# A batched matmul on one core: Tile's schedule against one critical section with waits by hand and a loop on TensorE

## The chip, the core and the metric

The kernel runs on one core of a Trainium2 chip. The metric is the time of one execution on the device in microseconds (us), the median of several runs. The profile is of one such execution; its span goes from the first instruction to the last.

## The reference

```python
batch, m, k, n = 32, 512, 1024, 768      # x: batch x m x k, weight: batch x k x n, float32

def reference(x, weight):
    return np.matmul(x, weight).astype(np.float32)
```

Each of 32 batches has its own x (512 x 1024) and its own weight (1024 x 768). There are 67 MB of x, 101 MB of weight and 50 MB of output in main memory, all in fp32.

## The kernel before

**The data.** A weight is cast to bf16 on its way in and lands as `w_sb` (128 partitions, 8 rows of 768 each; `load_w`, line 70). x lands in bf16 as well, two batches in one transfer (`load_pair`, line 60), so that 64 partitions hold one batch and 64 the other. Batch 0 and batch 31 are alone. Batch 0's x stays in fp32: three of its four row blocks come in one transfer of 1.5 MB on SP's queue (line 169, `x_first`). The fourth (`x_fourth`, 0.5 MB) comes in 18 transfers, four of 16 rows, two of 2 rows and twelve of 5 rows (line 172); the DMA completion semaphores make SP wait between them, so that they are issued from 1.2 to 29.3 us. There are four weight buffers, three x buffers (batch 0's `x_first` has one of them) and three output buffers. Batch 31's x is loaded by `load_last` (line 64).

**The work on a batch.** The contraction index must lie on the partitions, so TensorE (PE) first transposes x against an identity matrix, two bf16 values at a time as one fp32 word (`words`, line 78; `transpose_first`, line 113, for batch 0). VectorE (DVE) copies the result from the accumulator memory and sorts it by batch (`transpose_pair`, line 96; lines 93 and 94 for the last pair, 101 for batch 31, 115 for batch 0). A pair of batches has 8 groups of 4 transposes, with two accumulator buffers `pt` between PE and DVE. All 8 groups come ahead of the matmuls of the pair's first batch.

Then come 64 matmuls a batch (`matmuls`, line 132): for each of 4 row blocks, 8 steps of the contraction, each with 512 and 256 output columns. Two row blocks fill three accumulator banks (`pm`); there are two sets of three. When two row blocks are done, `evacuate` (lines 151 to 163) copies the banks to the output buffer: ScalarE (ACT) the first and the third, DVE the second, each in two halves of 64 partitions. A stored pair of batches, 3 MB, is one transfer.

**The one batch in parts.** `CHUNKED` holds batch 28 alone. Its weight comes in two transfers of half the contraction each, and its matmuls go through all four row blocks with the first half before they go through them with the second, in all six banks at once.

**The order.** The schedule is written out by hand (`manual_schedule`): the program order of each engine is that of the code, and the framework places the waits. Pool's queue issues all loads but the first x, and most stores. At batch b it issues, for odd b, the load of the pair that is three batches ahead and the store of an older pair, and for every b the weight of batch b+3, as soon as PE is done with batch b-1. The last stores (pairs 12 to 15) come late: two on Pool at batch 28, the others on SP at the very end, in halves for batches 30 and 31.

## Time and profile before

| | |
|---|---|
| median of 3 runs | 513.84 us (513.78 to 513.95) |
| the profiled execution | 513.74 us |
| its span | 511.9 us |
| PE busy | 425.1 us, 83% of the span |
| DVE, ACT busy | 171.8 and 145.4 us |
| TensorE clock granted, mean | 0.953 |
| HBM read, written | 167.77 and 50.33 MB, 426 GB/s over the span |
| queue of the Pool-issued transfers | 96.4% of 16 engines' span |
| first matmul of batch 0; of its last row block | 15.8 us; 45.9 us |

The slices in the DMA row are fortieths of the span, 12.8 us each, and a digit is the busy share in tenths, 9 for 90% or more. The GB/s row counts the bytes on the side of the core's memory: a load that casts fp32 to bf16 counts half of what is read. The clock row gives what the throttle granted to TensorE. A landing time runs from issue to the completion semaphore. In a timeline, the bracket behind a group is the idle time just ahead of it and what ended it.

### The profile page before, as it was taken

How to read it: one execution, taken by the hardware profiler on the slowest of the kernel's cores; microseconds unless marked ns; L12 is line 12 of the kernel's file. 1: busy time of each engine (PE TensorE's matmuls, PEld its weight loads, DVE VectorE, ACT ScalarE, POOL GpSimd, SP SyncE). 2: the span in 40 equal slices, each digit the busy share in tenths (PEclk: the TensorE clock that was granted, in tenths of full speed). 3: DMA queues.
4: the chain of work that ended last, by engine and by line, in shares of the span. 5: the costliest groups of instructions: out<-in, count | busy, mean ns of one | idle time of the engine just before them, and what ended most of it. 6: DMA issues, size and time to landing. Idle time of an engine off the chain costs nothing.

```text
span 511.9 us, 5954 instructions
## 1 busy us (share of the span) xinstructions
PE 425.1 (83%) x2528; PEld 276.6 (54%) x2576; DVE 171.8 (34%) x272; ACT 145.4 (28%) x249; POOL 34.3 (7%) x69
## 2 busy tenths in 40 slices
PE   1804998989898989997888878887888879898992
PEld 1503666665656665653656446464465645666661
DVE  0302426253525252431525315252152621615230
ACT  1200242414242423332242322323223232232310
POOL 3000010101010101000010000101001000010000
PEclk9956999999999999997999989999799998999997
DMA  8999999999999999999999999999999999999997
GB/s 238 224 222 214 220 217 217 335 221 317 235 223 331 216 327 229 230 325 220 329 224 242 313 223 333 217 253 300 219 338 215 266 289 219 333 219 217 325 428 338
DMA packets 10218, 135.65 MB, mean 265 GB/s; under 512 B 1232, under 2 KB 1232, under 8 KB 2128
## 3 DMA queue, kind: packets, MB, share of 16 engines
q0 software_dynamic: 9072, 126.88, 96.4%
q1 hardware_dynamic: 1120, 8.39, 4.1%
q8 instruction: 20, 0.33, 0.2%
q14 instruction: 6, 0.05, 0.0%
HBM read 167.77 MB, written 50.33 MB: 426 GB/s over the span
## 4 chain that ended last, share of the span: by engine, by line
PE 45%; DMA 37%; issue 9%; DVE 5%; another core or an unknown queue 1%; POOL 0%; SPq 0%; ACT 0%; POOLq 0%
PE pm L132 40%; DMA w_sb<-in_weight_dram 29%; DMA one_sb<-in_x_dram 8%; PE pt L78 5%; DVE xT L96 3%; DVE out_sb L163 1%; PE pt L113 0%; DVE xT L93 0%; POOL out_dram L182 0%; DVE xT L94 0%; DVE one_sb L155 0%; DVE xT L101 0%; ACT out_sb L156 0%; SPq L172 0%
## 5 line engine op out<-in xcount | busy, mean ns | idle before, releaser
L132 PE MATMUL pm<-w_sb,xT 128*128 128x256 bf16 (+1 forms) x2000 | 343.8, 330 | 24.8 <-DMA w_sb<-in_weight_dram 22.3
L132 PEld LDWEIGHTS <-xT 128*128 128x128 bf16 x2048 | 203.3, 99 | 160.6 <-issue 33.0
L163 ACT COPY out_sb<-pm 64x512 f32<-64x512 f32 x240 | 139.5, 581 | 339.4 <-PE pm L132 286.1
L163 DVE COPY out_sb<-pm 64x512 f32<-64x512 f32 x120 | 82.6, 688 | 267.7 <-PE pm L132 185.9
L78 PE MATMUL pt<-ident,x_sb 128*128 128x128 f32 x496 | 79.9, 302 | 21.7 <-DVE xT L96 19.7
L78 PEld LDWEIGHTS pt<-ident,x_sb 128*128 128x128 f32 x496 | 69.3, 209 | 32.9 <-DVE xT L96 27.7
L96 DVE COPY xT<-pt 128x1024 bf16<-128x1024 bf16 x112 | 72.2, 687 | 10.6 <-PE pt L78 10.2
L70 POOL DMA_DIRECT2D w_sb<-in_weight_dram x33 | 17.7, 536 | 403.0 <-PE pm L132 402.2
L113 PE MATMUL pt<-ident,one_sb 128*128 128x128 f32 x8 | 1.9, 422 | 20.5 <-DMA one_sb<-in_x_dram 20.5
L115 DVE CAST xT<-pt 128x256 bf16<-128x256 f32 x16 | 6.0, 441 | 35.3 <-PE pt L113 35.1
L113 PE MATMUL pt<-ident,x_sb 128*128 128x128 f32 x24 | 4.9, 363 | 10.9 <-DMA x_sb<-in_x_dram 10.4
L113 PEld LDWEIGHTS pt<-ident,one_sb 128*128 128x128 f32 x8 | 1.6, 218 | 20.8 <-issue 20.8
L113 PEld LDWEIGHTS pt<-ident,x_sb 128*128 128x128 f32 x24 | 3.9, 206 | 11.7 <-issue 10.4
L60 POOL DMA_DIRECT2D x_sb<-in_x_dram x15 | 8.1, 540 | 11.0 <-PE pt L113 11.0
L182 POOL DMA_DIRECT2D out_dram<-out_sb x14 | 7.5, 538 | 5.7 <-issue 4.8
L155 DVE COPY out_sb<-pm 128x512 f32<-128x512 f32 x2 | 1.4, 692 | 8.8 <-PE pm L132 8.8
L155 DVE COPY one_sb<-pm 128x512 f32<-128x512 f32 x2 | 1.4, 692 | 8.3 <-PE pm L132 8.3
L93 DVE COPY xT<-pt 128x512 bf16<-128x512 bf16 x8 | 3.4, 421 | 0.7 <-PE pt L78 0.7
L94 DVE COPY xT<-pt 128x512 bf16<-128x512 bf16 x8 | 3.3, 415 | 0.0
L154 ACT COPY out_sb<-pm 128x512 f32<-128x512 f32 x2 | 1.2, 587 | 6.5 <-PE pm L132 6.5
L101 DVE COPY xT<-pt 128x1024 bf16<-128x1024 bf16 x4 | 2.6, 685 | 0.2 <-PE pt L78 0.2
L156 ACT COPY one_sb<-pm 128x512 f32<-128x512 f32 x2 | 1.2, 587 | 4.2 <-PE pm L132 4.2
(10 smaller groups left out, 5.1 us busy)
## 6 DMA issues: line engine op xcount, KB each, us to landing
w_sb<-in_weight_dram POOLq DMA_DIRECT2D x31, 1536.0 KB, 40.2
out_dram<-out_sb POOLq DMA_DIRECT2D x14, 3072.0 KB, 51.3
x_sb<-in_x_dram POOLq DMA_DIRECT2D x15, 2048.0 KB, 47.1
out_dram<-out_sb SPq DMA_DIRECT2D x1, 3072.0 KB
x_sb<-in_x_dram SPq DMA_DIRECT2D x1, 1536.0 KB
w_sb<-in_weight_dram POOLq DMA_DIRECT2D x2, 768.0 KB, 50.4
out_dram<-one_sb SPq DMA_DIRECT2D x2, 768.0 KB
out_dram<-out_sb SPq DMA_DIRECT2D x2, 768.0 KB
```

The source lines that it names most:

```text
L60: nc.gpsimd.dma_start(out=xs[b], in_=pair_view[b // 2])
L70: nc.gpsimd.dma_start(out=ws[b][:, at:at + n, :], in_=w_view[b, :, at:at + n, :])
L78: nc.tensor.transpose(pt[:, j, :], pairs[:, mo, j::JT], ident)
L93: nc.vector.tensor_copy(both[:, 0, :, half], pt[:, :, 0])
L94: nc.vector.tensor_copy(in_rows[1][:, :, half::2, :], pt[:, :, 1])
L96: nc.vector.tensor_copy(both[:, :, :, half].rearrange("p b j i r -> p j b i r"), pt)
L113: nc.tensor.transpose(pt[:, i, :], rows[:, JT * h + i::KT], ident)
L115: nc.vector.tensor_copy(xT[:, 2 * h + j].rearrange("p (h i) r -> p r h i", h=2), pt[:, 2 * j:2 * j + 2].rearrange("p r (i h) -> p r h i", ...
L132: nc.tensor.matmul(pm[bank][:, at:at + size], xT[:, ko // 2, :, ko % 2], ws[b][:, ko, off:off + size], start=(ko == 0 and not (together an ...
L155: nc.vector.tensor_copy(o[:, 512:1024], pm[1])
L163: copy(mine[:, at:at + 512], pm[i][H * h:H * (h + 1)])
L182: nc.gpsimd.dma_start(out=two_view[at], in_=twos[at])
```

## The change

The whole program becomes one critical section, in which the framework places no waits; semaphores, buffers and waits are allocated and written by hand. In it:

- PE runs batches 1 to 28 in a loop of seven passes on the engine itself (`pe.Fori`), each over two pairs of batches. Batch 0, the last pair (29 and 30) and batch 31 stand outside. The other engines stay written out. Because a loop needs waits on constants, PE takes its counters down (`then_inc(s, -1)`, and -16 and -8 at the end of a pass), and SP waits for each landing and then raises one counter for weights and one for x (`landed`).
- `x_first` holds all four row blocks and comes in one transfer of 2 MB into the space of the third output buffer.
- `CHUNKED` is gone: weight 28 comes in one transfer and its batch runs like the others.
- There are two x buffers and not three, so the load of pair k waits until PE has transposed pair k-2.
- The third bank's copy is shared: ACT copies its first half, DVE its second (`out_on_dve`, last line).
- bf16 matmuls are given whole, with no separate weight load in the listing.
- The order of loads and stores on Pool and SP is the old one.

```diff
-    CHUNKED = {B - 4: (4, 4)}
+    GROUPS = 2 * MT
+    W_SLOTS, X_SLOTS, OUT_SLOTS = 4, 2, 3
+    LOOPS = (B - 4) // W_SLOTS
+    LOOPED = 2 * LOOPS
...
+    x_first = outs[2][:, :MT * K].rearrange("p (mo k) -> p mo k", mo=MT)
...
+    def load_w(b):
+        if b >= W_SLOTS:
+            pool.wait_ge(s_mm, mm_done(b - W_SLOTS))
+        pool.dma_start(out=ws[b % W_SLOTS], in_=w_view[b]).then_inc(s_w[b % W_SLOTS], 16)
+
+    def load_x(k):
+        if k >= X_SLOTS:
+            pool.wait_ge(s_pt, pt_done(k - X_SLOTS))
...
+    def take(s):
+        pe.wait_ge(s, 1).then_inc(s, -1)
+
+    def pair_on_pe(k, q):
+        b = 2 * k + 1
+        take(s_xr)
+        for g in range(GROUPS):
+            if GROUPS * q + g > 1:
+                pe.wait_ge(s_c, GROUPS * q + g - 1)
+            transpose(b, g)
+        for r in range(2):
+            take(s_wr)
+            for mt in range(MT):
+                at = 4 * q + 2 * r + mt // 2
+                if not r:
+                    pe.wait_ge(s_c, GROUPS * q + 2 * mt + 2)
+                pe.wait_ge(s_a, at + 1 + mt % 2)
...
+                    pe.wait_ge(s_d, at + 1 + mt % 2)
+                multiply(b + r, mt)
...
+        with pe.Fori(0, LOOPS):
+            for q in range(2):
+                pair_on_pe(q, q)
+            pe.wait_ge(s_c, 2 * GROUPS).then_inc(s_c, -2 * GROUPS)
+            pe.wait_ge(s_a, 9).then_inc(s_a, -8)
+            pe.wait_ge(s_d, 9).then_inc(s_d, -8)
+        pair_on_pe(LOOPED, 0)
...
+    def out_on_dve(b, p):
...
+        for piece in pieces(b, p, 1):
+            last = dve.tensor_copy(*piece)
+        last.then_inc(s_d, 1)
+        dve.tensor_copy(*pieces(b, p, 2)[1]).then_inc(s_dp, 1)
...
+    def landed(what, i):
+        slots, ready = what
+        sp.wait_ge(slots[i % len(slots)], 16 * (i // len(slots) + 1))
+        sp.sem_inc(ready, 1)
...
-        x_first = x_pool.tile([P, MT - 1, K], F32, name="x_sb")
-        x_fourth = one_pool.tile([P, 1, K], F32, name="one_sb")
-        nc.sync.dma_start(x_first, x_view[0, :, :MT - 1])
-        few = [slice(at, first + 20, 4) for first in (0, 20, 40) for at in range(first, first + 4)]
-        for rows in (slice(64, 80), slice(80, 96), slice(96, 112), slice(112, P), slice(60, 62), slice(62, 64), *few):
-            nc.sync.dma_start(x_fourth[rows, 0], x_view[0, rows, MT - 1])
...
+    with tc.tile_critical():
+        sp.dma_start(x_first, x_view[0]).then_inc(s_first, 16)
+        on_pool()
+        on_pe()
+        on_dve()
+        on_act()
+        on_sp()
+        clear_on_pool()
```

`clear_on_pool` waits for the stores issued by Pool and for SP to have issued the last one, and then resets the section's semaphores.

## The prediction

> **What bounds the kernel now.** I read the page first (the DMA row, the queues, the groups), then the chain that ended last in order of time, then the timelines of PE and SP around the end, and last the table by windows around PE's long waits.

> The page:

> ```profile
> DMA  8999999999999999999999999999999999999997
> GB/s 238 224 222 214 220 217 217 335 221 317 235 223 331 216 327 229 230 325 220 329 224 242 313 223 333 217 253 300 219 338 215 266 289 219 333 219 217 325 428 338
> q8 instruction: 20, 0.33, 0.2%
> x_sb<-in_x_dram POOLq DMA_DIRECT2D x15, 2048.0 KB, 47.1
> w_sb<-in_weight_dram POOLq DMA_DIRECT2D x2, 768.0 KB, 50.4
> ```

> The transfer engines are full from end to end. Slices of loads alone run at 217 GB/s (counted in the bf16 that lands), so one weight (1.573 MB) takes 7.25 us, one pair of x (2.097 MB) 9.7 us, and a stored pair (3.146 MB at twice the rate) 7.3 us: a pair of batches needs 2 x 7.25 + 9.7 + 7.3 = 31.5 us. x waits 47 us from issue to landing, so some 37 us of other work stand ahead of it in the queue.

> The chain of waits:

> ```profile
> 77.33 0.70 DVE out_sb L163
> 104.53 0.70 DVE out_sb L163
> ...
> 373.37 49.45 DMA w_sb<-in_weight_dram
> 422.81 0.14 issue
> 422.95 8.34 PE pm L132 x40
> ```

> With its data there, PE takes 104.53 - 77.33 = 27.2 us a pair, so it gains 4.3 us a pair on the transfers until it has caught up, near 230 us. From then on it waits for a weight, the last time at 422.95, for batch 26. After that it never waits for a transfer again.

> The timelines, PE and SP:

> ```profile
> 422.95 12.24 PE L132 MATMUL pm<-w_sb,xT 128*128 128x512 bf16 x63 [4.14 <-DMA w_sb<-in_weight_dram]
> 441.43 20.96 PE L132 MATMUL pm<-w_sb,xT 128*128 128x512 bf16 x125
> 462.23 1.12 PE L78 MATMUL pt<-ident,x_sb 128*128 128x128 f32 x8
> 498.46 5.53 SPq L232 DMA_DIRECT2D out_dram<-out_sb  x2
> ```

> Batches 27 and 28 run from 441.43 to 462.39 without a gap, 10.48 us each, so batch 28 starts at 451.9. The last store is issued at 503.66, and the packets of the stores end at 510.6. Alone, it would start 1.0 us after its issue (as the first x does, issued at 0.74, first packet at 1.75) and move 0.786 MB at the 428 GB/s of slice 39 in 1.9 us: done by 506.6. So the end is still the transfers', and PE's tail has **4.0 us of cover**.

> The table by windows, around two waits of PE:

> ```profile
> 326.00:331.00 5.00, 2.58 (x16) 1.58 (x17) 1.15 (x2) 1.15 (x2) 1.60 (x3) 1.00 1.05 221
> 422.00:428.00 6.00, 5.05 (x22) 2.68 (x23) 0.00 (x0) 0.63 (x2) 0.00 (x0) 0.72 1.00 214
> ```

> After a gap of 2.47 us (325.95 to 328.42) the clock stays at 1.00. After each of the four gaps of 3.9 to 4.5 us it falls, and batch 26 takes 12.1 us instead of 10.48: 1.6 us lost. In two of the four the half clock lasted twice as long, so a long gap costs 1.6 to 2.7 us.

> **The change, part by part.** The sum is made against the profiled execution: span 511.9, 513.74 in all, 0.1 below the median of 513.84.

> *First x in one transfer.* The bytes are the same. In the transfer records the twelve 5-row pieces fall on five of the 16 engines (11 or 12 packets of 4 KB there until 100 us, at most two on most of the others), while the first three instruction fetches fall on other engines. So in before each of 11 engines carries 4 rows of x_fourth and about 20/11 fetches of 0.93 us, each of the five some 16 rows. In after every engine carries 8 rows: +4 x 0.16 = 0.6 us on the 11, less on the five. PE can start at about 16 us (first x by 11, weight 0 by 15) instead of 44; that only means that it meets the transfers' pace at batch 4 instead of at 230 us, since weights cannot come sooner.

> *TensorE's loop.* The instruction fetches are 20 packets for 5,100 PE records, one per 256. The loop body has 640 of them and some 50 waits, 2.7 packets. Not shown by any run: whether a pass after the first fetches them again. If not, about 5 packets remain (the text is 1,300 long); if so, 7 x 3 to 7 x 5 plus 4, up to 39. On the 11 engines with 0.6 for x this gives (5 - 20) x 0.93/11 + 0.6 = -0.7 us, -1.0 with the present unevenness gone (the engines end from 507.9 to 510.6), and +1.2 with 27 packets (+2.2 with 39). I take **+1.2**, and keep both ends. The stall of a branch back has no row either. It is covered twice: the waits ahead of the branch are met when DVE has copied a bank 1.4 us into the last 5.2 us of matmuls, so up to 3.8 us of work are queued, and PE idles some 3.4 us a pair. If both covers are too small, PE only comes later to a weight, until 20 us of queued transfers are used up. The last branch back lies before batch 25; the exit falls through.

> [...]

> *Two x buffers.* The load of x for pair k+2 now waits for the transposes of pair k. In before it was issued at 326.77 for the pair transposed from 340 to 345.4, so it moves 19 us later, and on Pool the store and the weight of batch b+3 queue behind it, 6 us later than now (339.28 to about 346). The order in the queue is unchanged, and of the 37 us ahead of x 18 are left. Cost: nothing; once the cover is gone, one us per us, in every pair.

> *DVE takes half of the third bank.* Ahead of a pair's transposes DVE now copies three half banks instead of two: +0.69 us a pair (its L163 mean is 688 ns). Hidden while PE waits for weights (27.2 + 0.7 = 27.9 against 31.5), but on the path once after batch 28: **+0.7**.

> *No weight in parts.* The two halves of weight 28 were issued at 402.30 and 402.83 and landed 50.4 us later in the middle, that is at 453.0; they lie 3.6 us apart, so the second landed at about 454.8 and PE can act on it 0.2 to 0.5 us later. Before, batch 28 began at 451.9 on the first half. Now it waits for the whole: 455.3 - 451.9 = **+3.4**. The stretch before it is DMA paced, 31.5 - 27.9 = 3.6 us of waiting, between the 2.47 that keeps the clock and the 3.88 that loses it. A fallen clock costs **0 or 2.2** (middle of 1.6 and 2.7).

> *Waits by hand.* SP relays each landing to PE: +0.1 (its semaphore records take 17 to 28 ns, two hops). PE's other waits are met a half batch ahead. Entry and exit of the section each add a round of all engines; the round at the end of before takes 0.8 us (511.1 to 511.9), the one at the start under 0.1 beyond its slowest engine: 0 to 1.0, taken as +0.5. Pool's clearing lies beside the last stores.

> **The sum.** The last store is late by 1.2 + 3.4 + 0.7 + 0.1 = 5.4 us; 4.0 are covered; 1.4 remain, and 0.5 for the rounds: 1.9. The transfers' own path gives 1.2 to 1.4 + 0.5, the same. 513.84 + 1.9 = **515.7 us**. The terms' bounds carry this case from 514.7 to 516.9.

> **Rivals.**

> - *The clock falls ahead of batch 28* (fetches repeated): +2.2, 517.9. For it: 3.6 us is nearer to 3.88 than to 2.47. Against: a stall at the branch before batch 25 shortens the wait for 26 and shifts nothing at 28, and if the clock falls at 26 the wait at 28 shrinks to 2.
> - *The loop stays on the engine* (5 fetches, even engines), the case on the other side: the term is -1.0, so the last store is late by 3.2, within the cover. The transfers' own work ends 1.5 to 2.3 us sooner (ends at their mean, 509.2, less 15 x 0.93/16 = 0.9), but the last store ends at 506.6 + 3.2 = 509.8, 0.8 sooner than now, and 0.5 goes to the rounds: 513.84 - 0.3 = 513.5, no change. It decides where fetches stay below 13. With the clock's fall it gives 515.7.
> - *Weight loads no longer run ahead.* The listing of after shows no separate weight load beside a bf16 matmul. If each of a pair's 128 matmuls showed its 99 ns, a pair would cost 27.9 + 12.7 = 40.6 us, 9 over the transfers' pace: some 650 us. Against it: the transposes carry their loads in the same way, 209 ns each, and eight take 1.12 us, 140 ns each, so the load lies under the matmul before it.
> - *The transfer queue runs dry* behind the later x: decides at 18 us of PE delay, which nothing here brings; a gap of 2 us a pair would be 540.

> **How the numbers follow.** Fetches repeated 0.55 (clock kept 0.33, fallen 0.22), loop resident 0.39 (clock kept 0.23, fallen 0.16), the last two together 0.06. A measurement of this kernel can tell 0.2%, 1.03 us, from no change. Faster by more takes a quarter of the resident case with the clock kept, 0.06 (rounds at nothing and weight 28 early); the same takes the rest of it, 0.17, a fifth of the resident case with the clock fallen, 0.03, and a fifth of the forecast, 0.07; slower is left, 0.67. The range leaves out the last two rivals and the outer ends: 513.0 to 518.2.

> **What would show it.** Right: the DMA row full to the end; PE starting near 16 us and idle some 3.5 us at every even batch; a wait of 3 to 4 us for w28 near 452, where before has none; DVE's first spread of a pair 0.7 us later; the last store issued at 508 to 509. The count of instruction packets decides the loop (5, 20 or over 25), the PEclk of the window 450 to 460 the clock. Wrong: a DMA share under 1.0 between 20 and 500 us, a pair's matmuls over 21 us, or a last store before 505.

## The result, and the profile after

The changed kernel takes 514.77 us (median of 20 runs, 513.8 to 516.19), the kernel before 513.87 beside it (20 runs, 513.77 to 514.18). The ratio is 1.0016, 95% interval [1.0009, 1.0022]. So it is slower by 0.9 us, half of the 1.9 forecast, inside the forecast range, and its runs scatter over 2.4 us where those of before scatter over 0.4 (in the three groups of experiments below, before itself scatters over 1.4 to 1.5 us, 513.72 to 515.25). The interval leaves out 1, so the 0.16% is more than noise, but it lies just under the mark of 0.2% that the chances used, and the interval reaches over that mark. By the mark the result counts as the same, to which the forecast gave 0.27; slower had 0.67. The profiled execution took 515.67 us.

The page of the changed kernel: span, granted clock, transfer engines and the queue of instruction fetches.

```profile
span 513.5 us, 6063 instructions
PEclk9999999899998889999889999999899898898999
DMA  8999999999999999999999999999999999999995
q8 instruction: 5, 0.08, 0.1%
```

The transfer engines are as full as before (38 of the 40 digits are a 9 on both pages). Five instruction packets, not 20: they fall at 31, 55, 79, 478 and 495 us, so the first pass of the loop (its transposes begin at 31.1 us, those of the second at 87.2) fetched its body and the six after it fetched nothing.

The waits of PE (total, times, longest):

```profile
PE pt L153 <- DVE xT L233: 30.0, 35, 1.9
PE pm L134 <- PEq L157: 29.9, 13, 3.6
```

The first line holds the gap ahead of each pair's transposes, up to 1.9 us (before 1.0). The second is the wait for a weight at the even batches, from 1.2 to 3.6 us (PEq is PE's sequencer, which waits there for SP's word that the weight has landed).

The timeline of PE at the end (start, length, matmuls; in the bracket the idle time ahead and what ended it; 64 matmuls are a batch):

```profile
443.89 10.35 PE L134 MATMUL pm<-w,xT 128*128 128x256 bf16 x62
455.49 10.56 PE L134 MATMUL pm<-w,xT 128*128 128x512 bf16 x63 [1.25 <-PEq L157]
465.89 1.12 PE L153 MATMUL pt<-ident,x 128*128 128x128 f32 x8
468.93 1.41 PE L153 MATMUL pt<-ident,x 128*128 128x128 f32 x8 [1.92 <-DVE xT L232]
470.53 3.77 PE L153 MATMUL pt<-ident,x 128*128 128x128 f32 x16 [0.18 <-DVE xT L232]
474.44 20.75 PE L134 MATMUL pm<-w,xT 128*128 128x256 bf16 x125
```

Three lines of the same timeline of before, for the gaps ahead of the transposes of pairs 13 and 14 and the start of batch 29:

```profile
437.18 1.35 PE L78 MATMUL pt<-ident,x_sb 128*128 128x128 f32 x8 [1.03 <-DVE xT L96]
464.51 1.38 PE L78 MATMUL pt<-ident,x_sb 128*128 128x128 f32 x8 [1.17 <-DVE xT L94]
469.05 20.96 PE L132 MATMUL pm<-w_sb,xT 128*128 128x512 bf16 x125
```

The timeline of SP's queue at the end of the changed kernel:

```profile
503.99 5.46 SPq L115 DMA_DIRECT2D out_dram<-out  x2
```

Batch 28 starts at 455.49, 3.6 us later than before (451.9). The gap ahead of pair 14's transposes is 1.92 us (before 1.17), and the 16 transposes from 470.53 take 3.77 us because the clock is down (0.50 from 470.95 to 474.36 us in the trace's clock records). Batches 29 and 30 end 5.2 us later than before (474.44 + 20.75 = 495.19 against 469.05 + 20.96 = 490.01; by a missing record the start reads 0.2 too late). SP's last group, which issues the last two stores, ends at 509.45 instead of 503.99: 5.46 us late.

The table by windows (span, PE, weight loads, DVE, ACT, POOL, granted clock, DMA share, GB/s) says where the clock fell:

```profile
450.00:460.00 10.00, 8.70 (x54) 5.11 (x53) 3.06 (x5) 2.90 (x5) 1.60 (x3) 1.00 1.00 212
469.00:475.00 6.00, 5.67 (x28) 4.46 (x30) 4.89 (x14) 0.00 (x0) 0.00 (x0) 0.72 1.04 219
```

At full clock behind the wait for weight 28, where the forecast's rival put a fall; down at the transposes, where nothing was expected.

### The profile page after: what moved, and what is told of

Its sections match the earlier page's. It is cut to its first block, busy times and chain, and to the rows that moved or that the text cites. A ratio compares the mean times of both kernels' runs of the same rounds, so it can differ in the third digit from the quotient of the medians.

```text
span 513.5 us, 6063 instructions
## 1 busy us (share of the span) xinstructions
PE 430.2 (84%) x2528; PEld 280.2 (55%) x2576; DVE 209.6 (41%) x332; ACT 110.2 (21%) x189; POOL 33.7 (7%) x68
## 3 DMA queue, kind: packets, MB, share of 16 engines
q0 software_dynamic: 8928, 126.88, 96.1%
## 5 line engine op out<-in xcount | busy, mean ns | idle before, releaser
L134 PE MATMUL pm<-w,xT 128*128 128x256 bf16 (+1 forms) x2000 | 338.8, 328 | 32.8 <-PEq L157 29.9
L134 PEld LDWEIGHTS pm<-w,xT 128*128 128x128 bf16 x2048 | 202.2, 99 | 168.0 <-issue 40.8
L279 DVE COPY out<-pm 64x512 f32<-64x512 f32 x120 | 82.6, 689 | 252.4 <-PE pm L134 251.5
L265 ACT COPY out<-pm 64x512 f32<-64x512 f32 (+1 forms) x122 | 70.7, 580 | 300.6 <-PE pm L134 299.9
L153 PE MATMUL pt<-ident,x 128*128 128x128 f32 x496 | 87.3, 326 | 32.6 <-DVE xT L233 30.0
L153 PEld LDWEIGHTS pt<-ident,x 128*128 128x128 f32 x496 | 73.7, 210 | 45.6 <-DVE xT L233 39.3
L268 ACT COPY out<-pm 64x512 f32<-64x512 f32 (+1 forms) x62 | 35.8, 578 | 89.2 <-PE pm L134 89.2
L281 DVE COPY out<-pm 64x512 f32<-64x512 f32 x60 | 41.2, 686 | 0.0
L101 POOL DMA_DIRECT2D x<-in_x_dram x15 | 8.0, 532 | 274.0 <-PE pt L153 273.8
L92 POOL DMA_DIRECT2D w<-in_weight_dram x32 | 17.2, 538 | 125.6 <-PE pm L134 124.6
L153 PE MATMUL pt<-ident,out 128*128 128x128 f32 x32 | 6.9, 371 | 12.7 <-DMA out<-in_x_dram 12.5
L109 POOL DMA_DIRECT2D out_dram<-out x14 | 7.5, 536 | 1.4 <-DVE out L281 1.3
L232 DVE COPY xT<-pt 128x512 bf16<-128x512 bf16 x8 | 3.3, 415 | 0.0
## 6 DMA issues: line engine op xcount, KB each, us to landing
x<-in_x_dram POOLq DMA_DIRECT2D x15, 2048.0 KB, 29.6
out<-in_x_dram SPq DMA_DIRECT2D x1, 2048.0 KB, 11.4
out_dram<-one SPq DMA_DIRECT2D x2, 768.0 KB, 9.3
out_dram<-out SPq DMA_DIRECT2D x2, 768.0 KB, 4.3
```

The source lines that it names most:

```text
L92: pool.dma_start(out=ws[b % W_SLOTS], in_=w_view[b]).then_inc(s_w[b % W_SLOTS], 16)
L101: pool.dma_start(out=slot, in_=pair_view[k]).then_inc(s_x[k % X_SLOTS], 16)
L109: eng.dma_start(out=two_view[a], in_=outs[a % OUT_SLOTS]).then_inc(sem, 16)
L134: last = pe.matmul(pm[bank][:, at:at + size], xT[:, ko // 2, :, ko % 2], w[:, ko, off:off + size], start=(ko == 0), stop=(ko == KT - 1),)
L153: last = pe.transpose(pts[g % 2][:, i, :], rows, ident)
L265: last = act.copy(*piece)
```

## The experiments

Three theories. **Tail:** the time is the later of two ends, that of the transfer queue and that of PE's tail with its last store; the change makes the tail late by what batch 28's whole weight and DVE's extra copy cost. **Rounds:** the section's entry and exit cost what is left. **Clock:** half-clock stretches (a granted clock of 0.50 in the trace's clock records), in another place in each run, make the median and the scatter. Twelve kernels were run, in three groups of four; each group has its own runs of the kernel before beside it, and ratios are to these.

One table of the profiled executions carries most of the reading. The third column is the end of SP's last group in the SP timeline (its start plus its length), the last counts half-clock stretches that begin at a pair's transposes between 30 and 505 us in the trace's clock records.

| kernel | batch 28 starts | last group ends | span | span less that | falls at transposes |
|---|---|---|---|---|---|
| before | 451.9 | 503.99 | 511.9 | 7.9 | 0 |
| after | 455.49 | 509.45 | 513.5 | 4.05 | 7 |
| e5_after | 455.32 | 508.42 | 512.5 | 4.1 | 7 |
| e1_parts28 | 452.20 | 506.27 | 512.5 | 6.2 | 6 |
| e2_act_third | 455.84 | 510.83 | 514.9 | 4.1 | 0 |
| e3_unrolled | 456.48 | 509.58 | 513.7 | 4.1 | 8 |
| e4_warm | 455.40 | 510.40 | 514.5 | 4.1 | 11 |
| e6_act_warm | 455.49 | 509.31 | 513.4 | 4.1 | 1 |
| e7_act_parts | 452.48 | 506.21 | 511.9 | 5.7 | 1 |
| e8_act_parts_warm | 453.72 | 507.56 | 512.1 | 4.5 | 0 |
| e9_b_whole28 | 454.87 | 509.60 | 513.4 | 3.8 | 0 |
| e10_b_share | 453.1 | 506.61 | 512.0 | 5.4 | 5 |
| e11_b_whole_share | 455.00 | 509.46 | 513.3 | 3.8 | 3 |
| e12_act_warm_not30 | 455.80 | 508.31 | 512.5 | 4.2 | 0 |

The fifth column has two kinds of rows. Where the last group ends after 508 us, the span ends 4.05 to 4.2 us behind it (3.8 in kernels built on the one before). Where it ends earlier, the span stays at 511.9 to 512.5 whatever the group does: the transfer queue's end. That is the Tail theory's rule, and the cover of before is 7.9 - 3.8 = 4.1 us, where the forecast had 4.0. The queue's end itself varies by these 0.6 us, so the rows of e5 and e12, with spans of 512.5, fit the rule by their fifth column alone.

**One part undone: e1_parts28.** Batch 28's weight comes in two halves again, and its matmuls go through the row blocks twice; for that, six passes are in the loop, and the two pairs of the seventh are written out behind it.

```diff
-    LOOPS = (B - 4) // W_SLOTS
+    LOOPS = (B - 4) // W_SLOTS - 1
+    PARTS = B - 4
...
+        if b == PARTS:
+            for at in (0, JT):
+                pool.dma_start(
+                    out=ws[b % W_SLOTS][:, at:at + JT], in_=w_view[b, :, at:at + JT]
+                ).then_inc(s_part if at else s_w[b % W_SLOTS], 16)
+            return
```

> Weight 28 comes in two halves again, and batch 28 (outside the loop, which has six passes) goes through all row blocks with each half, as before the change. Tail theory (the last store is late by the wait for the whole of weight 28, 3.4 us, and by DVE's extra copy, 0.7, against 4.0 us of cover): batch 28 starts within 0.5 us of the end of batch 27, the last store is issued 2.5 to 3.5 us sooner, about 505.5, the transfers set the end again and, with 8 or so instruction packets instead of 20, the time is 513.0 to 513.5. Rounds theory (entry, exit and relays cost the 0.9 us, wherever PE stands): 514.8, as the change. Clock theory (falls of TensorE's clock in the tail cost it, the wait is only their cause): about 513.8, with the spread of the times halved.

Measured: 513.91 us (11 runs, 513.57 to 514.87), ratio 0.9994 [0.9985, 1.0003]. The timeline of its PE:

```profile
452.20 1.46 PE L170 MATMUL pm<-w,xT 128*128 128x512 bf16 x8
453.90 9.26 PE L170 MATMUL pm<-w,xT 128*128 128x256 bf16 x55 [0.23 <-issue]
463.00 1.11 PE L191 MATMUL pt<-ident,x 128*128 128x128 f32 x8
466.04 5.17 PE L191 MATMUL pt<-ident,x 128*128 128x128 f32 x24 [1.93 <-DVE xT L278]
```

No wait ahead of batch 28, while the gap of 1.93 us and the slow transposes (24 in 5.17 us) are still there. The loss is gone with this one part. Rounds, loop, two x buffers and shared bank together, what the loop spares counted in, cost no more than 0.03% (the interval's upper end), so the Rounds theory falls as a cause of the 0.9 us. The time itself does not part the other two: it misses the Tail theory's 513.0 to 513.5 by 0.4 us and lies at the Clock theory's 513.8. The profile does: the slow transposes still stand in the tail, their cost lies inside the cover.

**The same part done alone: e9_b_whole28**, on the kernel before.

```diff
-    CHUNKED = {B - 4: (4, 4)}
+    CHUNKED = {}
```

> The kernel before with one edit: batch 28's weight comes in one transfer, as in the changed kernel, so that it is waited for whole. Tail theory (the time is the later of two ends: the transfer queue's, at a span of about 511.9 us, and 4.1 us after the last store is asked for): batch 28 starts at about 455.4 us instead of 451.9, the last store is asked for at about 507.5 instead of 504.0, so 511.6, still within the cover: 513.7 to 514.2, no difference from before. If the wait of 3.5 us brings a half-clock stretch into the tail (1.2 us), 508.7 and a span of 512.8: 514.5 to 515.1. A rival by which the whole weight itself costs its wait: 517.

Measured: 514.73 us (12 runs, 513.94 to 516.98), ratio 1.0016 [1.0004, 1.0027]: the whole loss of the change, by one line. Its PE timeline:

```profile
454.87 13.12 PE L132 MATMUL pm<-w_sb,xT 128*128 128x512 bf16 x63 [4.26 <-DMA w_sb<-in_weight_dram]
467.83 1.12 PE L78 MATMUL pt<-ident,x_sb 128*128 128x128 f32 x8
470.12 1.38 PE L78 MATMUL pt<-ident,x_sb 128*128 128x128 f32 x8 [1.17 <-DVE xT L94]
```

The wait of 4.26 us loses the clock, and batch 28 behind it takes 13.12 us where 10.56 is the undisturbed length. So the last group is late by 3.0 (the start) plus 2.6 (the clock), 5.6 us. The 3.0 alone would stay within the cover of 4.1: in this kernel it is the fall of the clock behind the wait, itself brought by the wait, that takes the tail past it. The first value expected (no difference) was wrong; the second, with the clock's fall in the tail, held, and its price was too low (1.2 for 2.6).

**DVE's half of the third bank: e2_act_third, e10_b_share, e11_b_whole_share.** In the first, on the changed kernel, ACT copies both halves again and DVE writes one unread column to count:

```diff
-        act.copy(*pieces(b, p, 2)[0]).then_inc(s_ap, 1)
+        for piece in pieces(b, p, 2):
+            last = act.copy(*piece)
+        last.then_inc(s_ap, 1)
...
-        dve.tensor_copy(*pieces(b, p, 2)[1]).then_inc(s_dp, 1)
+        dve.memset(mark[:, j:j + 1], 0.0).then_inc(s_dp, 1)
```

> ACT copies both halves of the third bank again; DVE does only a 2-column write in its place to count. Tail theory: PE waits 1.03 us instead of 1.86 at a pair's third group, batch 29 starts 0.7 us sooner, the last store too, and the time is 0.5 to 0.7 below the change, 514.1. Rounds theory: 514.8. Clock theory: about 514.8 with the same spread, since the waits for weights become 0.7 us longer and the clock falls more often.

Measured: 514.11 us (12 runs, 513.65 to 517.08), ratio 1.0001 [0.9990, 1.0012]: the median is the Tail theory's 514.1, but the interval is too wide to tell it from either kernel. The profiled execution is the slowest of them, 517.08. Its PE timeline shows a stage like that of e9:

```profile
455.84 13.04 PE L135 MATMUL pm<-w,xT 128*128 128x512 bf16 x63 [3.90 <-PEq L158]
471.17 1.41 PE L154 MATMUL pt<-ident,x 128*128 128x128 f32 x8 [1.34 <-DVE xT L233]
```

PE is there earlier (no stretch at the transposes any more, gap 1.34), so it waits longer for the same weight, 3.90 us, and loses the clock there instead: 13.04 against 10.56. The share's cost had been hidden in that wait.

In the other two, on the kernel before, DVE takes the half; e11 also has e9's line.

```diff
             for h in range(2):
                 at = pair * N2 + h * MT * N + 512 * i
+                if i == 2 and h == 1:
+                    copy = nc.vector.tensor_copy
                 copy(mine[:, at:at + 512], pm[i][H * h:H * (h + 1)])
```

> The kernel before with one edit: VectorE copies the second half of the third bank, as in the changed kernel; weight 28 stays in halves. Clock theory: the gap ahead of each pair's transposes grows from 1.03 to about 1.86 us and half-clock stretches appear at the transposes, 5 or more in the profile. Tail theory: they cost the last store 0.8 us, or 2.0 with a stretch at pair 14, which is within the 3.8 us of cover, so 513.7 to 514.2, no difference. A rival by which half-clock stretches lengthen every stage: 515 or more.

> Both edits in the kernel before: whole weight 28 and the shared third bank; nothing else of the change (its rounds, its loop, its two x buffers and its first x are left out). Tail theory: 3.5 + 0.8 = 4.3 us late, 5.5 with a half-clock stretch at pair 14, so the last store at 508.3 to 509.5 and a span of 512.4 to 513.6: 514.2 to 515.4, slower than before although neither edit alone is. If the two edits do not add up to that, something else of the change makes it slower, and this stays at 513.7 to 514.1.

Measured: e10 514.26 us (11 runs), ratio 1.0004 [0.9996, 1.0013]; e11 515.08 us (11 runs, 513.62 to 516.51), ratio 1.0019 [1.0006, 1.0032]. PE in e10:

```profile
466.33 1.38 PE L78 MATMUL pt<-ident,x_sb 128*128 128x128 f32 x8 [1.78 <-DVE xT L94]
467.99 3.81 PE L78 MATMUL pt<-ident,x_sb 128*128 128x128 f32 x16 [0.28 <-DVE xT L94]
```

The share alone brings the longer gap (1.78) and the half clock at the transposes (16 in 3.81 us) into the kernel before, five times in this profile, and it costs nothing that can be measured: its last group ends at 506.61, inside the cover. Both edits together give the change's ratio again, inside the 514.2 to 515.4 expected; what the share adds to e9 lies within the intervals. In e11's profile the clock falls behind a wait for weight 28 of only 2.58 us, and batch 28 takes 12.24 us.

**The loop: e3_unrolled.** PE's seven passes are written out; nothing else differs.

```diff
-        with pe.Fori(0, LOOPS):
+        for _ in range(LOOPS):
```

> TensorE's seven passes are written out instead of looped, all else as in the change. Theory that the loop's body stays on the engine and spares 15 fetches: 20 instruction packets again, weights land up to 1 us later toward the end, and the time is 0.6 to 1.3 above the change, 515.4 to 516.1. Theory that the fetches are lost among 16 engines: 514.8. Theory that the branch back costs PE time: 514.0 or less.

Measured: 516.8 us (5 runs, 515.83 to 517.16), ratio 1.0048 [1.0035, 1.0061]. Its page has the fetches:

```profile
q8 instruction: 21, 0.34, 0.2%
```

Its PE timeline at batch 28:

```profile
456.48 10.56 PE L134 MATMUL pm<-w,xT 128*128 128x512 bf16 x63 [2.15 <-PEq L157]
```

With 21 packets instead of 5, batch 28 can start 1.0 us later (456.48 against 455.49), and the last group ends 1.2 us later than in e5, the profile of the change without a fall in the tail (509.58 against 508.42). In time the loop spares the change 1.5 us by the ratios to before and 1.9 by the medians, both against e5 on another chip. The median of 516.8 lies above the 515.4 to 516.1 expected; the profile, of the fastest of the five runs, does not show what the other 0.3 to 0.9 us are.

**The clock: e4_warm, e5_after, e6_act_warm, e12_act_warm_not30.** PE does 12 unread transposes ahead of each even batch's wait: on the changed kernel (e4), with ACT on the whole third bank (e6), and so but not ahead of batch 30 (e12, `if r and b + r < B - 2`). e5 is the changed kernel itself on e6's chip.

```diff
+    def idle_work():
+        for i in range(12):
+            pe.transpose(pts[0][:, i % JT, :], ident, ident)
...
+            if r:
+                idle_work()
```

> Ahead of the wait for each even batch's weight PE does 12 transposes of the identity that nobody reads (1.7 us of work; the result is unchanged). Clock theory: gaps ahead of even batches fall from 3.3 to about 1.6 us, the clock stays at 1.0 after them, the times lie within 0.5 us of each other and the median is 513.8 to 514.0. Tail theory without the clock: the wait for weight 28 ends when the weight lands, whatever PE does meanwhile, so 514.5 to 514.8, and the spread shrinks only as far as it came from the clock. Rounds theory: 514.8 and the same spread.

> The changed kernel itself again, as the control for the next three, on their chip. Both theories: between 513.8 and 516.2, median near 514.8, 5 instruction packets, wider from run to run than the kernel before, and in the profile half-clock stretches of 3.4 us both after waits for weights and at the pairs' transposes.

> ScalarE copies both halves of the third bank again (VectorE writes one column instead, to count) and TensorE does 12 unread transposes ahead of the wait for each even batch's weight. Clock theory (the change's spread and its median come from half-clock stretches, which start at two places: after long waits for weights, and at the pairs' transposes where the gap ahead of them is 1.86 us): with a gap of about 1.3 us at the transposes and the waits filled, no half-clock stretch is left between 30 and 505 us, the runs lie within 0.6 us of one another, and the median is 513.4 to 514.0. Tail theory (what counts is the wait for batch 28's whole weight and the store chain behind it, 5.4 us late against 4.0 of cover): the weight still lands where it landed, so the last store stays 4 to 5 us late and the time is 514.3 to 515.0 whatever the clock does.

> As the run with ScalarE on the whole third bank and unread transposes ahead of even batches, but with none ahead of batch 30, where no wait is left for them to fill and they put 1.3 us into the tail. Weight 28 stays whole. Tail theory: batch 28 starts at about 455.4 us as always, no half-clock stretch follows it, so the last store is asked for at about 508.0 (509.3 less 1.3) and the span is 512.1: 514.0 to 514.6, narrow. If the runs still lie above 515, something besides the filled work and the half-clock stretches moves the end from run to run.

Measured: e4 516.08 us (6 runs), ratio 1.0031 [1.0019, 1.0043]; e5 514.94 (12 runs, 514.06 to 516.49), 1.0019 [1.0009, 1.0029]; e6 516.16 (7 runs), 1.0034 [1.0022, 1.0046]; e12 514.67 (12 runs, 513.45 to 516.33), 1.0011 [1.0000, 1.0022]. e4 misses both of its expectations: its tail holds the share, a fall at pair 14 and the unread transposes ahead of batch 30. e6 lies above both of its own, 513.4 to 514.0 and 514.3 to 515.0. The PE timeline of e5:

```profile
455.32 10.56 PE L134 MATMUL pm<-w,xT 128*128 128x512 bf16 x64 [1.60 <-DVE out L279]
468.75 1.41 PE L153 MATMUL pt<-ident,x 128*128 128x128 f32 x8 [1.93 <-DVE xT L232]
```

The view puts this wait down to DVE, whose copy of batch 27's last banks the first matmuls of batch 28 do not need; the last piece of weight 28 landed at 454.99, 0.33 us ahead of the start (in after at 455.17, 0.32 ahead).

The same of e6, with the unread transposes ahead of batch 30:

```profile
455.49 10.56 PE L135 MATMUL pm<-w,xT 128*128 128x512 bf16 x64 [2.59 <-PEq L158]
483.18 1.47 PE L163 MATMUL pt<-ident 128*128 128x128 f32 x12
484.49 10.56 PE L135 MATMUL pm<-w,xT 128*128 128x512 bf16 x64
```

And of e12:

```profile
455.80 10.56 PE L135 MATMUL pm<-w,xT 128*128 128x512 bf16 x63 [2.59 <-PEq L158]
468.65 1.41 PE L154 MATMUL pt<-ident,x 128*128 128x128 f32 x8 [1.34 <-DVE xT L240]
```

In these and in after batch 28 starts between 455.3 and 455.8, whatever PE did ahead of it. From there to the end of the last group it is 52.5 us in e12 (no fall, no share), 53.1 in e5 (no fall, with the share: +0.6), 54.0 in after (the share and a fall at pair 14: +0.9) and 55.0 in e2 (a fall behind the wait: +2.5). e6 has no fall in the tail and is still late, since the transposes ahead of batch 30, 484.49 - 483.18 = 1.3 us, have no wait to fill; without them e12 is 1.5 us faster, by medians from two chips. That was a fault of the experiment's design, but it reads near to the rule that beyond the cover a microsecond in the tail is a microsecond of the time.

The changed kernel's loss does not need the clock: in e5's profile no fall lies in the tail, and the span is still 0.6 us over before's. That no part of the median comes from the clock is not shown. e12 stays above before, but its interval begins at 1.0000, and its profile is not like its other runs: it has the highest granted clock of the twelve, 0.990, where the others have 0.979 to 0.985, so they had falls that it lacks. A fall in the tail costs 0.9 or 2.5 us in these profiles, and whether there is one changes from profile to profile, so the clock is one part of the scatter. e12 was expected narrow and is not: seven of its 12 runs lie from 514.5 to 516.3. How much of that is falls in the tail, and what else moves its end, is open.

**Two versions meant to beat both: e7_act_parts (e1 and e2 together) and e8_act_parts_warm (with e6's transposes too).**

> ScalarE copies both halves of the third bank, and batch 28's weight comes in two halves again (six pairs of batches in the loop, two written out); waits are not filled. Tail theory: the wait ahead of batch 28 (3.6 us) and VectorE's share of the delay (0.8 us) are both gone, so the last store is less than 1 us later than before and the time is set by the transfer queue: 513.2 to 513.9. Clock theory: the same median, with falls after waits for weights alone and none in the last 60 us, as weight 28 is not waited for; runs up to 1 us above that where a fall lies at batch 24 or 26.

> All three together: third bank to ScalarE, batch 28's weight in two halves, 12 unread transposes ahead of each even batch's wait. Both theories: the end is set by the transfer queue alone, 513.0 to 513.7 with a spread under 0.6 us, faster than the changed kernel by about 1 us and equal to the kernel before or 0.3 us faster. If the clock matters beyond the tail (batches end sooner, stores are asked for sooner), it is below e7 by 0.2 to 0.5 us; if not, the same as e7.

Measured: e7 513.73 us (11 runs, 513.36 to 514.35), ratio 0.9995 [0.9986, 1.0003]; e8 514.02 (11 runs, 513.66 to 514.63), 0.9999 [0.9990, 1.0008]. e7 is 1.2 us faster than the changed kernel on that chip, with less than half of its scatter, and not to be told from the kernel before: both end with the transfer queue. e8 was expected at or below e7, 513.0 to 513.7, and is above; its transposes ahead of batch 30 took 1.3 us of the cover, and its last group (507.56) ends just where the cover does.

## Where the prediction was right, and where not

- **Cover.** Forecast 4.0 us, measured 4.1. The rule behind it, that only lateness beyond the cover counts, holds in all fourteen rows of the table, to within the 0.6 us by which the queue's end varies. Right, and it is why e9 and e11 cost time and e1, e7 and e10 do not.
- **Weight 28 waited for whole.** Forecast: start at 455.3 without the fetch term. Measured 455.49 and 455.32. Right in size, and shown as the cause of the loss by e1 (undone, the loss is gone) and e9 (done alone, it is there). How the tail gets past the cover differs: in the change by this wait with the share's 0.6 behind it, in e9 by this wait with a fall of the clock. The wait itself was 1.25 to 1.6 us, not 3 to 4: PE came to it at 454.24 and not at 452, held up by the longer gaps and the falls of the clock ahead of it. That changes nothing, as the landing sets the start.
- **DVE's copy.** Forecast +0.69 in the gap and +0.7 in the tail; measured 1.86 against 1.03 in the gap (+0.83) and +0.6 in the tail. Right. What was missed is that with the longer gap the clock falls at the transposes: 7 times in after and 5 in e10, never in before.
- **The fetch term, +1.2: the step that failed.** Its condition, a body fetched again in every pass, is not met, and no run shows the term: there were 5 packets in seven passes, and weight 28 landed 0.3 to 0.5 us later. By the forecast's formula 5 packets give -0.7 and e3's 21 give +0.7. The semaphore records have the last piece of weight 28 landing at 454.69 in before, at 455.17 and 454.99 in the changed kernel's two profiles, and at 456.16 in e3: +0.3 to +0.5 with 5 packets, +1.5 with 21. So 16 packets moved the landing by 1.0 to 1.2 us; 16 x 0.93 spread over 16 engines is 0.9, over the forecast's 11 it is 1.4. But both kernels lie 0.8 to 1.2 us above the formula. In sum the term was +0.3 to +0.5. Something of the change other than fetches makes the weight late by that much; which part is not shown. That e3 starts batch 28 at 456.48, where the forecast's terms give 456.6, is therefore luck. The rival that had the loop resident was right that the passes after the first fetch nothing, and wrong about the gain, -0.7 to -1.0. Its -1.0 supposed even transfer engines, and in the transfer records of after the 16 engines still end their part of the last pair stores of Pool's queue from about 493 to 496.3 us (before from about 494 to 497.6).
- **The clock.** The rival put the fall behind the wait for 28, at 2.2 us. e9 and e2 show that fall at 2.5 to 2.6, e11 at 1.7; in the changed kernel's two profiles it does not occur, and one has a fall at pair 14 instead, 0.9 us, which no step contained. The forecast's reading that 2.47 us keeps the clock and 3.88 loses it does not hold: e9 has both outcomes for a gap of 2.47 (last section), and in e2 a gap of 3.90 us ahead of 329.8 us kept it.
- **The sum.** 5.4 us late was forecast and 5.46 measured, but the agreement is partly luck: 1.2 for fetches did not come, and 0.9 for the clock and some 0.4 of small gaps did. Where no fall lies in the tail (e5's profile) the lateness is 4.4. Without the fetch term the forecast's own sum is 4.2 - 4.0 + 0.5 = 0.7 over before, close to the measured 0.9.
- **The rounds.** Forecast +0.5. First issue at 0.96 instead of 0.74 us, and 4.1 instead of 3.8 from the last group to the end: +0.5 in a run that the tail ends. In size right. Another 0.2 us lies outside the span and was in no term: the changed kernel's times are 2.0 to 2.1 us above its spans (medians of its two series), before's 1.8. In runs that the queue ends (e1, e7) nothing of the 0.5 is seen in the time.
- **Not needed.** No weight load came out from under the matmuls (128x512 and 128x256 take 384 and 275 ns on average, before 387 and 277), and the queue did not run dry (96.1% of 16 engines' span, before 96.4%).

## What to carry to other kernels

Measure the cover at the end first: how much later may the last store be asked for before the time moves? Edits that fit into it cost nothing alone and all of what exceeds it together, so each has to be costed against what the others leave. Where a landing sets a start, work saved or lost ahead of it is not seen (batch 28 started at 455.3 to 455.8 us with and without the unread transposes); the same work behind it counts in full once the cover is used up, as the 12 unread transposes ahead of batch 30 did (1.3 us of tail in e6's profile).

## What was not expected of the hardware

- A loop body of 640 PE records ran seven times on 5 instruction packets in all; written out, the same work took 21, and 1.5 to 1.9 us more (e3 against e5).
- Half-clock stretches at transposes. The kernels with a gap of 1.65 to 1.93 us ahead of a pair's transposes show 3 to 11 of them in a profile; those with a gap of 1.03 to 1.34 show none or one (e7's, at pair 14, follows a gap of 1.34). The transposes behind that gap are short, eight in 1.35 us, with gaps of 0.2 to 0.3 between the groups, so no single gap is long. In after PE was busy for 0.4 to 1.8 of the 3.41 us ahead of each of its eleven half-clock stretches, in before for 0.9 us at most ahead of its four. A sparse stretch alone does not settle it: in after PE was busy for 1.43 of the 3.41 us from 324.17, and the clock stayed at 1.00; and of 15 pairs, all but the last with a gap of 1.86 or 1.87 us, seven show a fall.
- No length of a gap decides it. In e9's profile two waits of 2.47 us stand ahead of the same work, and one loses the clock:

```profile
265.39 12.24 PE L132 MATMUL pm<-w_sb,xT 128*128 128x512 bf16 x63 [2.47 <-DMA w_sb<-in_weight_dram]
423.24 10.56 PE L132 MATMUL pm<-w_sb,xT 128*128 128x512 bf16 x63 [2.47 <-DMA w_sb<-in_weight_dram]
```
